# Turning mLSTM score blocks two steps behind instead of one, in banks of their own

## The chip, the cores and the metric

The kernel runs on one core of a Trainium2 chip. Five engines work side by side, each through its own line of instructions, in order: TensorE (PE in the profile, its weight loads PEld), VectorE (DVE), ScalarE (ACT), GpSimd (POOL) and SyncE (SP, which issues most DMAs). [...] Data lies in SBUF; TensorE writes to PSUM, which has eight banks of 128 partitions by 512 fp32 numbers. The metric is the device time of one launch in microseconds.

## The reference

One hybrid encoder block on 512 tokens of width 1024, all in fp32. RMSNorm, one wide projection, then three mixers side by side (a bidirectional mLSTM with 4 heads of 128, a neighbourhood attention, a cross-attention into 256 memory tokens), a gated merge, an output projection and a gated FFN. The change lies in the mLSTM. For one head and one direction it computes, with log gates `log_f`, `log_i` and their running sums `a` in a chunk:

```
m_j = max(a + m_prev, max_s D)          # D = a_j - a_s + log_i_s, causal
P = exp(D - m_j) * (q k^T)
inter_w = exp(a + m_prev - m_j)
num = P v + inter_w * (C_prev q)
den = sum(P) + inter_w * (n_prev q)
h = num / max(|den|, exp(-m_j))
```

The state `C, n` goes from chunk to chunk. A second scan runs on the reversed sequence, the two results are added, normalised over the head's 128 columns (RMS), scaled by a gain and gated by `sigmoid(o)`.

## The kernel before, in words

**Numbers and matmuls.** A product of two fp32 matrices is made from high and low parts: `mm3` (L212 to L215) issues three fp32r matmuls (high by high, high by low, low by high) into one PSUM bank. Weights come by DMA into `wr`, ACT copies the high part (`wh`, L195) and DVE subtracts to get the low part (`wl`, L196). A projection `proj` of 8 weight tiles is 24 matmuls of 512 columns. Transposes and a few small products are plain fp32.

**The mLSTM beside the projections.** TensorE has a stream of projections (memory query, output gate, memory keys and values, neighbourhood queries and keys, merge gates). The mLSTM is a generator, `ml_all`; a piece of it, up to the next `yield`, is set into the stream at places that a quota decides: each projection adds `RB`, `RM`, `RN` or `RATE` steps to it (L29, L30), a quarter of it at a time after some of its weight tiles. `late` is a list of functions which the next projection calls after its second, fourth or sixth tile (`flush`). Python's order gives priorities; Tile's scheduler then makes each engine's line from them, moving work that is ready earlier. `tc.issue_after(ins)` forbids it to put what is traced inside ahead of `ins` on that engine.

**A head.** The sequence is four blocks J of 128 tokens, both directions at once. `keys` (next head) transposes k into PSUM (L681), splits keys and queries into high and low (L689 to L694, tiles `u`) and puts `weigh` into `late`, which scales the values by their gate weights: `ew` by DVE (L699), high parts by ACT (L702), low parts by DVE (L703). `states` multiplies keys by weighted values into two banks (L721 and L213 to L215 with `at<-u`), then makes the running states C with ACT (L733) and DVE (L735) and splits them (L219, L220). Then come four steps `weights_J`, J = 0 to 3:

- scores q by k (L755) into columns 384 to 511 of a bank `ps`, and q by C (L763 for J = 0 and 3, three fp32r matmuls for J = 1 and 2) into columns 0 to 257 of the same bank;
- DVE multiplies the exponentials `E` by the scores and sums them (L771), makes the denominator and its reciprocal (L774 to L776), and mixes both directions into `ee` (L777, L778);
- the part from the state goes to H: ACT takes the first direction (L784), DVE adds the second (L786). Both read the bank `ps`.

The mixed block must be transposed before it meets the values. `turn_J` (TensorE L794, copy by ACT L795) does so inside the next block's `weights_J`, straight behind that block's scores; it writes columns 384 to 511 of its own block's bank `ps`. `values_J` (TensorE L800, DVE L801, squares by ACT L803) does the product with the values at the start of the step after, into the same columns. After a head's last block `normalise` takes the root (DVE L807, POOL L809) and four ACT scalings (L814), and `emit_y` transposes the head's H (L822), multiplies by the gate (DVE L824) and splits (L219, L220) for the branch product.

**Buffers.** PSUM is split in two pools of four banks: `mm` (projections, and the transposed keys) and `at` (blocks, states, transposed H and others). DVE and ACT also make every `wl` and `wh`, in the same lines as the mLSTM's work.

The functions as they were:

Of the kernel before, what the change touches and what calls it, by code (L numbers as in the profile page):

```python
# [17 lines left out]
P = 128  # L18
S = 512
# [9 lines left out]
WARM = 14  # L29
RM, RB, RN = 0.7, 1.25, 1.35  # L30
RATE = 1.0
# [79 lines left out]
def hybrid_block(ctx, tc, xg, xT, memT, wflat, vecs, gbias, nabias, outa, outb, outc):  # L111
# [27 lines left out]
    def mmps():  # L139
        return mmp.tile([P, 512], F32, tag="mm", name=nm("mm"))  # L140
# [519 lines left out]
    def ml_all():  # L660
# [15 lines left out]

        def keys(h, R, ee):

            pt = mmps()
            for J in range(NT):  # L680
# [10 lines left out]
            qs = qT[:, h * S + P:h * S + 3 * P]  # L691
            A.activation(q[0], qs, AF.Copy)
            V.tensor_tensor(q[1], qs, q[0].bitcast(F32), op=ALU.subtract)
            A.activation(ke[:, :2 * P].rearrange("p (j c) -> p j c", j=2), pt.rearrange("p (j c) -> p j c", j=4)[:, 0:4:3, :], AF.Copy)  # L694

            def weigh():
                wt = ml["wt"]
                for d in range(2):
                    V.tensor_scalar(ew[d], va[:, 3 * d, h, 0:129], wt[:, d, 3 * d, h:h + 1], None, op0=ALU.mult)  # L699
                    for j in range(2):  # L700
                        ds, col = slice(129 * d, 129 * d + 129), wt[:, d, j + 1, h:h + 1]
                        A.activation(wh[j][:, ds], va[:, j + 1, h, 0:129], AF.Copy, scale=col)  # L702
                        st["dve"] = V.scalar_tensor_tensor(wl[j][:, ds], va[:, j + 1, h, 0:129], col,  # L703
                                                           wh[j][:, ds].bitcast(F32), op0=ALU.mult,
                                                           op1=ALU.subtract).ins

# [3 lines left out]
        def states(h, k, w, C, q, R, ee):  # L710
# [3 lines left out]
            (ke, kh, kl), (ew, wh, wl) = k, w  # L714
            pc = [atps() for _ in range(2)]
            po = (0, 130, 0, 131)
# [31 lines left out]
        def weights_J(H, ss, h, J, k, w, C, q, R, ee):  # L748
# [6 lines left out]
            PE.matmul(kq, qT[:, hs], kT[:, hs], start=True, stop=True)  # L755
            if open_J:
                turn_J(*open_J[0])
            if len(ds) == 2:
# [23 lines left out]
            for d in ds:  # L782
                if src is None:
                    A.activation(H[:, js], pi[:, d, 0:128], AF.Copy, scale=r[:, d:d + 1])  # L784
                else:
                    V.scalar_tensor_tensor(H[:, js], pi[:, d, 0:128], r[:, d:d + 1], src, op0=ALU.mult, op1=ALU.add)  # L786
                src = H[:, js]
            if J < NT - 1:
                exps(h, J + 1, R)
            return H, ss, h, J, E, ps  # L790

        def turn_J(H, ss, h, J, E, ps):
            pt = ps[:, 384:512]
            PE.transpose(pt, E[:, 0, :], ident)  # L794
            A.activation(E[:, 1, :], pt, AF.Copy)  # L795

        def values_J(H, ss, h, J, E, ps):
            js = slice(J * P, (J + 1) * P)
            pv = ps[:, 384:512]
            PE.matmul(pv, E[:, 1, :], va[:, J, h, 0:128], start=True, stop=True)  # L800
            V.tensor_tensor(H[:, js], pv, H[:, js], op=ALU.add)  # L801
            sq = scr(128)
            A.activation(sq, H[:, js], AF.Square, accum_out=ss[:, J:J + 1])  # L803

        def normalise(H, ss):
# [4 lines left out]

            def scale():
                for J in range(NT):
                    js = slice(J * P, (J + 1) * P)
                    A.activation(H[:, js], H[:, js], AF.Copy, scale=rs[:, J:J + 1])  # L814

            late.append(scale)

        def emit_y(h, H):
            pt = atps()
            for J in range(NT):  # L820
# [8 lines left out]

        prev = None  # L830
        open_J, ahead = [], []

        def keyed(h):
            return keys(h, nxt, tp.tile([P, S], F32, tag="H", name=nm("ee"), bufs=4))

# [3 lines left out]
        for h in range(4):  # L839
            if prev:  # L840
                values_J(*open_J.pop(0))
                turn_J(*open_J[0])
            states(h, *st_h)
# [9 lines left out]
            yield  # L853
            if prev:
                values_J(*open_J.pop(0))
                normalise(*prev)
            last = prev
            prev = tp.tile([P, S], F32, tag="H", name=nm("H"), bufs=4), tiny(4)
            open_J.append(weights_J(*prev, h, 0, *own))
            yield  # L860
            for J in range(1, NT):
                if J > 1:
                    values_J(*open_J.pop(0))
                if J == 2 and last:
                    emit_y(h - 1, last[0])
                open_J.append(weights_J(*prev, h, J, *own))
                if J == 3 and h < 3:
                    st_h = keyed(h + 1)
                if J < 3 and h < 3:
                    late.append(lambda d=J - 1, n=nxt, i=st["mix"]: mask(n, d, i))  # L870
                yield
        values_J(*open_J.pop(0))
        turn_J(*open_J[0])
        yield
        values_J(*open_J.pop(0))
        normalise(*prev)
        flush()
        yield
# [654 lines left out]
```

## Time and profile before

| what | value |
|---|---|
| median of three runs | 875.74 us (875.68 to 875.85) |
| the profiled execution's own time | 876.06 us |
| its span in the trace | 874.3 us |
| lying around the span (start and end) | 1.8 us |
| granted TensorE clock | 0.999 |
| mLSTM's blocks on TensorE | from 128 us to 240 us of the span |

A row of the timeline has the start and the duration in us, engine, line, operation, tiles (out<-in), shape and count, and in brackets idle time of the engine before it with what ended it. TensorE's matmuls are pipelined and the profile models their ends, so rows overlap: the time that TensorE gives to an instruction is read from start to start. In the page's first part each engine has its busy time, the share of the span and the number of instructions.

### The profile page before, as it was taken

What the parts mean: (1) busy time and instruction counts of PE and PEld (TensorE: products, weight loads), DVE (VectorE), ACT (ScalarE), POOL (GpSimd) and SP (SyncE); (2) the same over time, 40 slices, a digit from 0 to 9 for tenths busy, and PEclk for the clock granted to TensorE, in tenths of its full rate; (3) what the DMA queues carried; (4) which work ended last, traced back from release to release, by engine and by line L of the source; (5) the groups of instructions that cost most, each with busy time, mean ns of one, the idle gap of its engine ahead of it and who ended that gap; (6) DMA issues with size and microseconds to landing.
All of it is one profiled execution on the core that took longest, in us unless ns stands there. A gap on an engine that the chain in (4) does not pass through costs nothing.

```text
span 874.3 us, 12280 instructions
## 1 busy us (share of the span) xinstructions
PE 868.3 (99%) x4287; PEld 734.8 (84%) x4287; DVE 600.8 (69%) x1332; ACT 469.8 (54%) x989; POOL 124.9 (14%) x201
## 2 busy tenths in 40 slices
PE   9999999999999999999999999999999999999997
PEld 7898888888888888888888888888888888888887
DVE  6794698987577758897676558776633466666534
ACT  7563567765456658888544455444422344444532
POOL 0101100000073470700000002111100011111010
PEclk9999999999999999999999999999999999999999
DMA  8324644522352453633223432322233322232412
GB/s 280 101 73 146 200 138 120 171 73 87 107 126 86 107 165 109 157 117 125 97 97 109 144 109 96 98 96 97 76 100 101 110 97 97 96 97 91 134 42 97
DMA packets 39422, 99.82 MB, mean 114 GB/s; under 512 B 5688, under 2 KB 13880, under 8 KB 39360
## 3 DMA queue, kind: packets, MB, share of 16 engines
q1 hardware_dynamic: 31568, 92.32, 32.5%
q0 software_dynamic: 7360, 6.32, 3.5%
q8 instruction: 34, 0.56, 0.3%
q10 hardware_dynamic: 432, 0.39, 0.1%
q14 instruction: 28, 0.23, 0.1%
HBM read 94.80 MB, written 4.21 MB: 113 GB/s over the span
## 4 chain that ended last, share of the span: by engine, by line
PE 95%; DVE 2%; ACT 1%; issue 1%; POOL 0%; POOLq 0%; ACTq 0%; DVEq 0%
PE mm L213 28%; PE mm L214 28%; PE mm L215 28%; PE at L214 2%; PE at L213 2%; PE at L215 2%; PE at L961 1%; PE at L942 1%; PE at L923 0%; PE at L924 0%; PE at L1049 0%; PE at L800 0%; DVE wl L196 0%; PE at L243 0%; PE at L794 0%
## 5 line engine op out<-in xcount | busy, mean ns | idle before, releaser
L213 PE MATMUL mm<-u,wh 128*128 128x512 f32 (+1 forms) x1072 | 414.7, 387 | 0.0
L214 PE MATMUL mm<-u,wh 128*128 128x512 f32 (+1 forms) x1072 | 412.0, 384 | 0.0
L215 PE MATMUL mm<-u,wl 128*128 128x512 f32 (+1 forms) x1072 | 411.8, 384 | 0.0
L195 ACT ACTIVATE wh<-wr 128x512 fp32r<-128x512 f32 (+2 forms) x298 | 183.9, 621 | 204.1 <-PE mm L214 161.1
L196 DVE TENSOR_TENSOR wl<-wr,wh 128x512 fp32r<-128x512 f32 (+3 forms) x300 | 204.2, 682 | 89.9 <-ACT wh L195 87.7
L215 PEld LDWEIGHTS mm<-u,wl 128*128 128x128 f32 x1072 | 201.5, 188 | 40.2 <-DVE wl L196 0.2
L214 PEld LDWEIGHTS mm<-u,wh 128*128 128x128 f32 x1072 | 201.8, 188 | 38.6 <-DVE u L220 0.3
L213 PEld LDWEIGHTS mm<-u,wh 128*128 128x128 f32 x1072 | 201.7, 188 | 38.4
L1397 POOL TENSOR_TENSOR s<-s,rb 128x512 f32<-128x512 f32 x22 | 38.0, 1730 | 402.7 <-DVE s L1396 239.0
L540 POOL DMA_DIRECT2D u<-nav_d x128 | 62.2, 513 | 64.7 <-PE at L961 22.9
L219 ACT ACTIVATE u<-s 128x512 fp32r<-128x512 f32 x26 | 16.4, 633 | 57.8 <-DVE s L1400 56.2
L1400 DVE TENSOR_TENSOR s<-mm,s 128x512 f32<-128x512 f32 x22 | 15.2, 691 | 23.9 <-POOL s L1397 23.9
L460 ACT ACTIVATE s<-pad,vec 128x512 f32<-128x512 f32 x30 | 24.4, 813 | 9.7 <-DVE pad L458 9.7
L220 DVE SCALAR_TENSOR_TENSOR u<-s,u 128x512 fp32r<-128x512 f32 x26 | 19.1, 734 | 13.5 <-ACT u L219 13.3
L461 DVE SCALAR_TENSOR_TENSOR s<-pad,vec,s 128x512 f32<-128x512 f32 x30 | 22.5, 750 | 5.5 <-ACT s L460 5.5
L1396 DVE SCALAR_TENSOR_TENSOR s<-s,s 128x512 f32<-128x512 f32 x22 | 15.2, 692 | 13.4 <-ACT s L1395 13.3
L462 DVE SCALAR_TENSOR_TENSOR s<-pad,vec,s 128x512 f32<-128x512 f32 x30 | 22.5, 750 | 0.9
L1395 ACT ACTIVATE s<-s 128x512 f32<-128x512 f32 x22 | 13.9, 632 | 14.9 <-DVE s L1394 14.9
L458 DVE TENSOR_TENSOR pad<-mm,rb 128x512 f32<-128x512 f32 x22 | 15.1, 690 | 6.4 <-PE mm L215 6.2
L1175 DVE TENSOR_TENSOR s<-mm,rb_x 128x512 f32<-128x512 f32 x16 | 11.0, 689 | 12.1 <-PE mm L215 12.0
L1407 DVE TENSOR_TENSOR u<-mm,u 128x512 f32<-128x512 f32 x13 | 9.0, 692 | 14.6 <-PE mm L215 14.6
L213 PE MATMUL mm<-wh,u 128*128 128x512 f32 x48 | 18.8, 392 | 0.0
(338 smaller groups left out, 1074.0 us busy)
## 6 DMA issues: line engine op xcount, KB each, us to landing
wr<-wflat SPq DMA_DIRECT2D x141, 512.0 KB, 3.4
nab<-nabias SPq DMA_DIRECT2D x16, 256.0 KB, 2.7
u<-nav_d POOLq DMA_DIRECT2D x128, 32.0 KB, 2.9
s<-xT SPq DMA_DIRECT2D x15, 256.0 KB, 4.0
wr<-wflat SPq DMA_DIRECT2D x14, 192.0 KB, 2.4
nav_d<-nv POOLq DMA_DIRECT2D x8, 256.0 KB, 2.5
R<-rd SPq DMA_DIRECT2D x8, 256.0 KB, 5.4
wr<-wflat SPq DMA_DIRECT2D x2, 544.0 KB, 3.4
```

The costliest lines, as they stand in the source:

```text
L195: A.activation(h[:, u:v], src, AF.Copy)
L196: V.tensor_tensor(l[:, u:v], src, h[:, u:v].bitcast(F32), op=ALU.subtract)
L213: PE.matmul(ps, lh, rh, start=start, stop=False)
L214: PE.matmul(ps, lh, rl, start=False, stop=False)
L215: st["mm"] = PE.matmul(ps, ll, rh, start=False, stop=stop).ins
L219: A.activation(h, src, AF.Copy, scale=scale)
L220: V.scalar_tensor_tensor(l, src, scale, h.bitcast(F32), op0=ALU.mult, op1=ALU.subtract)
L460: A.activation(t1, pad[:, 0:512], AF.Identity, scale=vcol(w, i), bias=vcol(b, i))
L461: V.scalar_tensor_tensor(t1, pad[:, 1:513], vcol(w, n + i), t1, op0=ALU.mult, op1=ALU.add)
L462: V.scalar_tensor_tensor(t1, pad[:, 2:514], vcol(w, 2 * n + i), t1, op0=ALU.mult, op1=ALU.add)
L540: G.dma_start(vw[r * 32:(r + 1) * 32, i * 256:(i + 1) * 256], nav_v[hf, r, CW[b]:CW[b] + 32, hp * 256:(hp + 1) * 256])
L1397: G.tensor_tensor(c, c, rb2, op=ALU.mult)
```

## The change

`turn_J` no longer takes the last block. A counter `clock` goes up with every step of the generator after the first; each block is kept with the count at which it was made, and is turned when it is at least two counts old. `values_J` follows one step behind the turn. A turned block gets an `at` bank of its own (transpose in columns 0 to 127, values in 128 to 255) and no longer uses the scores' bank. The banks of `states` and of `emit_y` come from `mm` in place of `at`. `normalise` moves from the next head's J = 0 to its J = 1 and `emit_y` from J = 2 to J = 3, where it stands ahead of the next head's `keys`; the four scalings of H are put behind J = 1's L784 (now L789) on ACT. The next head's split of the queries and its scalings are kept behind places of J = 1: on ACT behind that same L789, on DVE behind J = 1's last mix (L778, now L783). The generator has one step more at its end, and `RN` goes from 1.35 to 1.475, over 8 projections one step more. No instruction is added or taken away on any engine.

```diff
-RM, RB, RN = 0.7, 1.25, 1.35
+RM, RB, RN = 0.7, 1.25, 1.475
...
-        def keys(h, R, ee):
+        def keys(h, R, ee, act=None, dve=None):
+
+            behind = lambda ins: tc.issue_after(ins) if ins else nullcontext()
...
-            A.activation(q[0], qs, AF.Copy)
-            V.tensor_tensor(q[1], qs, q[0].bitcast(F32), op=ALU.subtract)
+            with behind(act):
+                A.activation(q[0], qs, AF.Copy)
+            with behind(dve):
+                V.tensor_tensor(q[1], qs, q[0].bitcast(F32), op=ALU.subtract)
...
-                    V.tensor_scalar(ew[d], va[:, 3 * d, h, 0:129], wt[:, d, 3 * d, h:h + 1], None, op0=ALU.mult)
+                    with behind(dve):
+                        V.tensor_scalar(ew[d], va[:, 3 * d, h, 0:129], wt[:, d, 3 * d, h:h + 1], None, op0=ALU.mult)
...
+                        with behind(act):
+                            A.activation(wh[j][:, ds], va[:, j + 1, h, 0:129], AF.Copy, scale=col)
+                        with behind(dve):
+                            st["dve"] = V.scalar_tensor_tensor(wl[j][:, ds], va[:, j + 1, h, 0:129], col,
...
-            pc = [atps() for _ in range(2)]
+            pc = [mmps() for _ in range(2)]
...
-            if open_J:
-                turn_J(*open_J[0])
+            turn_J()
...
-            return H, ss, h, J, E, ps
-
-        def turn_J(H, ss, h, J, E, ps):
-            pt = ps[:, 384:512]
-            PE.transpose(pt, E[:, 0, :], ident)
-            A.activation(E[:, 1, :], pt, AF.Copy)
-
-        def values_J(H, ss, h, J, E, ps):
+            open_J.append((H, ss, h, J, E, clock[0]))
+
+        def turn_J():
+            if open_J and clock[0] - open_J[0][-1] > 1:
+                *blk, _ = open_J.pop(0)
+                E = blk[-1]
+                pt = atps()
+                PE.transpose(pt[:, :P], E[:, 0, :], ident)
+                A.activation(E[:, 1, :], pt[:, :P], AF.Copy)
+                turned.append((*blk, pt))
+
+        def values_J():
+            if not turned:
+                return
+            H, ss, h, J, E, pt = turned.pop(0)
             js = slice(J * P, (J + 1) * P)
-            pv = ps[:, 384:512]
+            pv = pt[:, P:2 * P]
...
         def emit_y(h, H):
-            pt = atps()
+            pt = mmps()
...
+            for J in range(NT):
+                values_J()
+                scale = normalise(*last) if J == 1 and last else None
+                weights_J(*prev, h, J, *own)
+                if scale:
+                    late.append(lambda f=scale, i=st["inter"]: f(i))
+                if J == 1:
+                    ins = st["inter"], st["mix"]
+                if J == 3:
+                    if last:
+                        flush()
+                        emit_y(h - 1, last[0])
+                    if h < 3:
+                        st_h = keyed(h + 1, *ins)
+                if J in (1, 2) and h < 3:
+                    late.append(lambda d=J - 1, n=nxt, i=st["mix"]: mask(n, d, i))
+                yield
+                clock[0] += 1
```

The engines' lines differ only inside the mLSTM's stretch, on TensorE, DVE and ACT; SP's line is the same row for row, and POOL's differs in the place of one clearing of a buffer (L888).

Three places show what moved. In the rows `mm` and `at` are PSUM banks, `u_149` and its like hold the projections' inputs, `u_455` and `u_456` the queries and keys, the other `u` the split keys, queries and weighted values of a head, `ee` the mixed blocks.

TensorE, last head, J = 1: one projection's last matmul, the block's scores, and what stands behind them. Before:

```order
L215 MATMUL mm_2480<-u_147,wl_2379 128x512
L755 MATMUL at_2497<-u_456,u_455 128x128
L794 MATMUL at_2446<-ident,ee_2340 128x128
L213 MATMUL at_2497<-u_2346 128x258
L214 MATMUL at_2497<-u_2346 128x258
L215 MATMUL at_2497<-u_2346 128x258
L213 MATMUL mm_2480<-u_149,wh_2382 128x512
```

Now:

```order
L215 MATMUL mm_2484<-u_147,wl_2415 128x512
L812 MATMUL at_2443<-u_595,ee_2031 128x128
L761 MATMUL at_2499<-u_456,u_455 128x128
L213 MATMUL at_2499<-u_2327 128x258
L214 MATMUL at_2499<-u_2327 128x258
L215 MATMUL at_2499<-u_2327 128x258
L213 MATMUL mm_2484<-u_147,wh_2414 128x512
```

The turn of block 0 (L794, into block 0's own bank `at_2446`) is gone from this step; it stands in J = 2's, and here the values product (L812) of the head before it has come in.

DVE, second head, J = 3, from the low part of the keys (L690, now L691) to the last scaling for the next head's states (L703, now L709). Before:

```order
L690 TENSOR_TENSOR u_2035<-mm_2030,u_2035 128x256
L774 SCALAR_TENSOR_TENSOR y_2018<-y_2018 128x2
L196 TENSOR_TENSOR wl_2055<-wr_1971,wh_2054 128x512
L775 TENSOR_TENSOR y_2018<-y_2018,em 128x2
L699 TENSOR_SCALAR s_2036<-u_595,wt 128x129
L776 RECIPROCAL y_2018<-y_2018 128x2
L703 SCALAR_TENSOR_TENSOR u_2035<-u_595,wt,u_2035 128x129
L777 TENSOR_SCALAR ee_1632<-E_1968,y_2018 128x128
L780 TENSOR_TENSOR y_2018<-num,y_2018 128x1
L196 TENSOR_TENSOR wl_2059<-wr_1971,wh_2058 128x512
L778 SCALAR_TENSOR_TENSOR ee_1632<-E_1968,y_2018,ee_1632 128x128
L703 SCALAR_TENSOR_TENSOR u_2035<-u_595,wt,u_2035 128x129 x2
```

Now, from the split of the head's gated output (L220) on:

```order
L220 SCALAR_TENSOR_TENSOR u_2028<-s_2025,u_2027 128x512
L780 TENSOR_TENSOR y_2003<-y_2003,em 128x2
L196 TENSOR_TENSOR wl_2057<-wr_1955,wh_2056 128x512
L781 RECIPROCAL y_2003<-y_2003 128x2
L691 TENSOR_TENSOR u_2037<-mm_2032,u_2037 128x256
L782 TENSOR_SCALAR ee_1628<-E_1952,y_2003 128x128
L785 TENSOR_TENSOR y_2003<-num,y_2003 128x1
L696 TENSOR_TENSOR u_2037<-u_455,u_2037 128x256
L783 SCALAR_TENSOR_TENSOR ee_1628<-E_1952,y_2003,ee_1628 128x128
L196 TENSOR_TENSOR wl_2061<-wr_1955,wh_2060 128x512
L709 SCALAR_TENSOR_TENSOR u_2037<-u_595,wt,u_2037 128x129 x4
L813 TENSOR_TENSOR H_1796<-at_1999,H_1796 128x128
```

Before, one of the four scalings and the queries' low part stood some 18 rows ahead of this piece, in J = 2; now all four and the queries' low part (L696) stand here, behind the gated output's two DVE operations, which were in J = 2.

ACT, the same place. Before, from the gated output's high part (L219) on:

```order
L219 ACTIVATE u_1945<-s_1943 128x512
L692 ACTIVATE u_2035<-u_455 128x256
L702 ACTIVATE u_2035<-u_595,wt 128x129 x3
L195 ACTIVATE wh_1995<-wr_1912 128x512
L195 ACTIVATE wh_1999<-wr_1912 128x512
L702 ACTIVATE u_2035<-u_595,wt 128x129
L1142 ACTIVATE u_1645<-mm_1866,rc_m 128x512
```

Now:

```order
L219 ACTIVATE u_2027<-s_2025 128x512
L195 ACTIVATE wh_2056<-wr_1955 128x512
L690 ACTIVATE u_2037<-mm_2032 128x256
L694 ACTIVATE u_2037<-u_455 128x256
L1158 ACTIVATE u_1641<-mm_1859,rc_m 128x512
L195 ACTIVATE wh_2060<-wr_1955 128x512
L697 ACTIVATE s_2038<-mm_2032 128x256
L789 ACTIVATE H_1796<-at_1997,y_2003 128x128
L707 ACTIVATE u_2037<-u_595,wt 128x129 x4
```

Before, the scalings (L702) were made in J = 2, ahead of the next keys; now the four (L707) are the last of ACT's work in J = 3.

61 lines of the change are left out of this document (23 added, 38 removed).

## The prediction

> **What bounds the kernel.** I read the page's first part and its chain first, then the view of what the turn (L794) and TensorE's other instructions waited for, and last TensorE's timeline, row by row, in the stretch that the change reorders. The first part and the chain:
>
> ```profile
> PE 868.3 (99%) x4287; PEld 734.8 (84%) x4287; DVE 600.8 (69%) x1332; ACT 469.8 (54%) x989; POOL 124.9 (14%) x201
> ...
> PE 95%; DVE 2%; ACT 1%; issue 1%; POOL 0%; POOLq 0%; ACTq 0%; DVEq 0%
> ```
>
> TensorE is busy for 868.3 of 874.3 us, and the chain that ends last is 95% its own work. The change takes no instruction from TensorE, so it can win only what TensorE stands still, and only where the order differs, from 128 to 240 us. It can lose wherever DVE or ACT get something TensorE needs later than now. The view of L794 gives what ended the idle time before it (us, times; the weight load's idle time counts too, which can lie beside the matmul before it):
>
> ```profile
>   ACT H L784: 1.4, 4
>   DVE H L786: 0.6, 2
> ```
>
> Six of 16 turns find the bank occupied, for 2.0 us in all, and each time it is the reading of H that ends the wait. The view of TensorE's waits adds one for the first head's product with the state:
>
> ```profile
> PE at L763 <- DVE C L735: 0.3, 1, 0.3
> ```
>
> Together 2.3 us: the upper bound of what there is to win. Why a turn waits is seen at the first of them, in DVE's and ACT's rows:
>
> ```profile
> 132.92 0.35 DVE L778 SCALAR_TENSOR_TENSOR ee<-E,y,ee 128x128 f32<-128x128 f32 x1
> ```
>
> ```profile
> 134.73 0.35 ACT L784 ACTIVATE H<-at,y 128x128 f32<-128x128 f32 x1
> ```
>
> The mixed block was finished at 133.27, but ACT read the bank for H until 135.08, and the turn, which writes to other columns of that bank, begins at 135.13. So the input was 1.86 us early, and the bank was late.
>
> **The gain, from start to start.** How much TensorE itself lost I take from the distance between an instruction ahead of the wait and the one behind it, against the same pair where nothing was late. The first is the product with the state, L755 to the projection's L213 behind L763, late and then undisturbed:
>
> ```profile
> 128.20 0.38 PE L755 MATMUL at<-u,u 128*128 128x128 f32 x2
> ...
> 129.11 0.48 PE L213 MATMUL mm<-u,wh 128*128 128x512 f32 x1
> ...
> 155.38 0.39 PE L755 MATMUL at<-u,u 128*128 128x128 f32 x2
> ...
> 155.75 0.36 PE L213 MATMUL mm<-u,wh 128*128 128x256 f32 x1
> ```
>
> 0.91 against 0.37: 0.54 us lost. The turns, with an undisturbed one at 142.06 and another at 217.10:
>
> ```profile
> 134.74 0.40 PE L213 MATMUL mm<-u,wh 128*128 128x512 f32 x1
> 135.13 0.33 PE L794 MATMUL at<-ident,ee 128*128 128x128 f32 x1
> 135.22 0.48 PE L214 MATMUL mm<-u,wh 128*128 128x512 f32 x1
> ...
> 141.84 0.39 PE L215 MATMUL mm<-u,wl 128*128 128x512 f32 x1
> 142.06 0.39 PE L213 MATMUL mm<-u,wh 128*128 128x512 f32 x1
> ...
> 142.32 0.47 PE L214 MATMUL mm<-u,wh 128*128 128x512 f32 x1
> ...
> 149.93 0.28 PE L214 MATMUL at<-u 128*128 128x258 f32 x1
> ...
> 150.28 0.37 PE L215 MATMUL at<-u 128*128 128x258 f32 x1
> ...
> 171.69 0.40 PE L214 MATMUL mm<-wl,u 128*128 128x512 f32 x1
> ...
> 172.18 0.47 PE L215 MATMUL mm<-wh,u 128*128 128x512 f32 x1
> ...
> 211.12 0.38 PE L755 MATMUL at<-u,u 128*128 128x128 f32 x2
> 211.81 0.32 PE L794 MATMUL at<-ident,ee 128*128 128x128 f32 x1 [0.31 <-ACT H L784]
> 211.89 0.37 PE L213 MATMUL at<-u 128*128 128x258 f32 x1
> ...
> 217.10 0.39 PE L755 MATMUL at<-u,u 128*128 128x128 f32 x2
> ...
> 217.35 0.36 PE L213 MATMUL at<-u 128*128 128x258 f32 x1
> ...
> 222.12 0.39 PE L755 MATMUL at<-u,u 128*128 128x128 f32 x2
> ...
> 222.66 0.39 PE L763 MATMUL at<-C,u 128*128 128x129 f32 x2
> ```
>
> - 134.74: 0.48 against 0.26 (142.06 to 142.32): 0.22.
> - 149.93: 0.35. Undisturbed it would be half of the 0.22 that a 512-column matmul takes (141.84 to 142.06), since it has 258 columns, and 0.04 for a turn (0.26 less 0.22), so 0.15: 0.20 lost.
> - 171.69: 0.49 against 0.26: 0.23.
> - 211.12: 0.77 against 0.25 (217.10 to 217.35): 0.52.
> - 222.12: 0.54 against the same 0.25: 0.29.
>
> The turns make 1.46 and the state 0.54, 2.00 in all. The sixth turn is not among them, and the two views allow 2.3; I take 2.1, nearer to the rows.
>
> **The change, part by part.** *Own banks, two steps.* With a bank of its own the turn (L802) waits for no reading of H, so all turn waits go. It now stands a step later than its mix; a step is 6.0 us (211.12 to 217.10), so the mix, which was 1.86 us early at the first turn, has that on top. Each step takes two of the `at` pool's four banks, so a bank comes round after two steps, 12 us after its block's scores, and H's reading, some 6 us behind them now, does not hold it. What the values (L812) wait for, ACT's copy (L803), is a step old again: nothing. The copies, sums and squares are as many as before; each moves by a step on an engine that isn't the bound: nothing, beside the place below.
>
> *The state's product of the first head.* In the new order projections lie between the states and L768, enough to cover the 0.29 of waiting. The opposite holds for the third head, where a projection's matmuls go from ahead of L768 (18 to 12, six by 0.22, 1.3 us). The rows of that wait:
>
> ```profile
> 179.76 0.34 DVE L735 SCALAR_TENSOR_TENSOR C<-C,dec,at 128x129 f32<-128x129 f32 x1
> ```
>
> ```profile
> 177.23 0.28 PE L214 MATMUL at<-u 128*128 128x258 f32 x1
> ...
> 182.03 0.39 PE L763 MATMUL at<-C,u 128*128 128x129 f32 x2
> ```
>
> The state is complete at 180.10 and used at 182.03: 1.93 early, 0.6 after the change. I put 0 (to 0.3).
>
> *Tied scalings and the later gated output.* This is the place where the change can cost. For the third head's states, the scalings (DVE's L703, now L709, and ACT's L702, now L707) come last in the second head's J = 3 now, behind the gated output, which was made a step earlier. DVE's rows for what has come ahead of the last scaling, for a mask (L675), and for the last scaling:
>
> ```profile
> 166.31 0.75 DVE L824 SCALAR_TENSOR_TENSOR s<-at,ngh,u 128x512 f32<-128x512 f32 x1
> ...
> 167.75 0.69 DVE L220 SCALAR_TENSOR_TENSOR u<-s,u 128x512 fp32r<-128x512 f32 x1
> ...
> 168.90 0.42 DVE L693 TENSOR_TENSOR u<-u,u 128x256 fp32r<-128x256 f32 x1
> ...
> 169.31 0.35 DVE L703 SCALAR_TENSOR_TENSOR u<-u,wt,u 128x129 fp32r<-128x129 f32 x1
> ...
> 172.02 0.68 DVE L675 TENSOR_TENSOR R<-R,msk 128x512 f32<-128x512 f32 x1
> ...
> 175.94 0.61 DVE L703 SCALAR_TENSOR_TENSOR u<-u,wt,u 128x129 fp32r<-128x129 f32 x2
> ```
>
> Rows of one engine overlap by some 0.08 us (175.94 plus 0.61 is 176.55; the row behind it begins at 176.47), so the first four cost 0.67, 0.61, 0.34 and 0.27: 1.89 us more ahead of the last L709. It ended at 176.55, and the states' matmul that reads it, the L214 above at 177.23, was 0.68 behind: at worst TensorE waits 1.89 less 0.68, 1.2 us. Against it stands the mask: in the trace it lies in J = 3 behind the mix, now it stands ahead of J = 3's first operation, in time that DVE has while the scores are still to come; that gives back up to 0.60 and leaves 0.6 us. How much DVE stands still in these steps is in the windows view (us, then busy time and count of PE, PEld, DVE, ACT, POOL, then clock, DMA share, GB/s):
>
> ```profile
> 172.00:198.00 26.00, 25.99 (x139) 22.16 (x139) 23.80 (x88) 17.53 (x51) 1.04 (x1) 1.00 0.28 95
> ```
>
> DVE is idle for 2.2 of 26 us, which is 0.5 in a step of 6.0 us; ACT for 8.5, 2.0 in a step, so DVE is the later of the two. Idle time of 0.5 us against 0.6 us leaves a wait of 0.1, or of 0.6 where none of it falls in the right place. I take 0.3, between them; the ends for the range are 0 and 1.2.
>
> ACT's row shows what the worst end would come from:
>
> ```profile
> 167.09 0.63 ACT L219 ACTIVATE u<-s 128x512 fp32r<-128x512 f32 x1 [0.44 <-DVE s L824]
> ```
>
> ACT stood 0.44 us at L219 for DVE's product, and what stood behind it had to stand too. [...]
>
> *Banks of the `mm` pool.* The states' two banks and the transposed H now come from the projections' four. A bank is given back when its last reader is done: a projection's first matmul in the second head's J = 3 now waits until ACT has read the first half of the memory values (L1158). Between the last matmul of that half and the projection stand six matmuls of 0.22, the block's scores and eight transposes, well over 1.3 us, and an ACT operation of 512 columns takes 0.63 (L219 above): nothing. The states' banks are held from 177.5 (the L214 above, ended) to 180.10, 2.6 us; the projection behind them begins later than that. I put nothing, and up to 2.6 us each at three heads for the rival below.
>
> *RN, the further step, POOL and SP.* TensorE's instructions stay the same, only spread differently; SP's order is the same, and one clearing on POOL moves, which is busy for 14%: nothing.
>
> **Sum.** 2.1 won, 0.3 lost: 1.8 us less. The profiled execution took 876.06 us (span 874.3 and 1.8 around it), 0.3 above the median of the runs, and becomes 874.3; against the median, 875.74 less 1.8 is 873.9. About 0.2%, 1.75 us, is what a measurement can tell from no change, so this forecast lies on that edge.
>
> **The rivals.**
> - *A, the forecast:* 1.75 to 2.3 us less, 873.4 to 874.0. For it: the six waits all end with a reading of the bank that the turn no longer uses.
> - *B, the preparation comes late:* the third head's states wait the whole 1.2 us, and its product with the state 0.3; 2.1 less 1.5 leaves 0.6, 875.1 (with smaller shares of it 874.0 to 875.6). [...] For it: DVE is the fuller engine, 92% in these steps. Against it: the mask and the 0.5 us of idle time.
> - *C, nothing is won:* TensorE wins the turns and then stands at the next late operand, a low part of weights (L196 on DVE), since DVE has the same work to do in less time. The 1.8 would come back but for some 0.2: 875.5. For it: the same 92%. Against it: in the page's costliest groups the loads of L215, which take what L196 makes, waited for it only 0.2 us in the whole span (the last column), though DVE was as full in these steps before:
>
> ```profile
> L215 PEld LDWEIGHTS mm<-u,wl 128*128 128x128 f32 x1072 | 201.5, 188 | 40.2 <-DVE wl L196 0.2
> ```
>
> - *D, slower:* the `mm` pool becomes the bound. A projection that wants the bank the states hold stands until the last L741 has read it. At three heads, half of 2.6 us on the mean is 3.9; less the 1.8 it is 2.1 slower, 877.8. It decides from 1.2 us per head, where the loss passes 3.55 (1.8 and 1.75). For it: its four banks now carry the projections in flight, two states, the keys and H. Against it: the states' matmuls stand in the middle of a projection, 12 matmuls of 0.22, 2.6 us, ahead of the next one's begin.
>
> **How the numbers follow.** A 0.52, B 0.26, C 0.09, D 0.13. A alone is faster by over 0.2%: 0.52; B and C lie within it: 0.35; D slower: 0.13. The range reaches from A's lower end, 873.4, over B and C to 875.7, which leaves out D and the fringes; A's own range is 873.4 to 874.0.
>
> **What would show it.** Right: no idle time ahead of L802 for an ACT or DVE reading of H; L768 of the first head without its 0.29; TensorE's rows between 128 and 240 us shifted by 1.8. Wrong, B: idle time at the states' L213 or L214 ended by L707 or L709 around 176. Wrong, D: idle time at a projection's first L213, ended by L741, L739 or L837. Wrong, C: idle time at L215 ended by L196.

## The result and the profile after

| | before | after |
|---|---|---|
| median, run side by side | 875.80 us (875.68 to 876.27, 13 runs) | 873.78 us (873.43 to 874.44, 13 runs) |
| ratio, 95% interval | | 0.9978 (0.9969 to 0.9986) |
| profiled execution, span | 876.06, 874.3 us | 873.57, 871.8 us |

The change wins 2.0 us, 0.22%; 1.8 were forecast. The page's first part and the chain of the changed kernel:

```profile
PE 866.4 (99%) x4287; PEld 734.3 (84%) x4287; DVE 601.1 (69%) x1332; ACT 470.9 (54%) x989; POOL 124.9 (14%) x201
...
PE 98%; DVE 1%; issue 0%; ACT 0%; POOL 0%; POOLq 0%
```

DVE and ACT do the same work; the chain, 95% TensorE before, is 98% TensorE now. The view of what the turn waited for (L802) has no line under its heading, where that of L794 had 2.0 us:

```profile
its engine sat idle before it (us, times) until:
who waited for it (us, times):
```

To see how much of it belongs to the reordered stretch, I take two instructions of TensorE that stand outside it in both kernels: L612's four transposes ahead of it, and the first eight transposes of the neighbourhood attention behind it (L1049, now L1065). Before, in TensorE's timeline:

```profile
116.16 0.51 PE L612 MATMUL at<-ident,s 100*128 100x100 f32 x4
...
252.90 1.03 PE L1049 MATMUL at<-ident,s 128*128 128x128 f32 x8
```

After:

```profile
115.38 0.51 PE L612 MATMUL at<-ident,s 100*128 100x100 f32 x4
...
250.38 1.03 PE L1065 MATMUL at<-ident,s 128*128 128x128 f32 x8
```

136.74 us before, 135.00 after: 1.74 us. Of the 2.5 us by which the two spans differ, another 0.78 lie ahead of L612, where both kernels have the same rows; behind L1065 nothing is left (621.4 in both). The experiments are compared by this "stretch". Each kernel has one trace, so how well a stretch repeats is not measured; the piece behind it, which has the same instructions in every kernel here, takes 621.4 us in all 14 traces.

Three of the places after. The first head's product with the state, and the turn of 211 us:

```profile
127.42 0.38 PE L761 MATMUL at<-u,u 128*128 128x128 f32 x2
127.56 0.48 PE L213 MATMUL mm<-u,wh 128*128 128x512 f32 x1
...
128.34 0.45 PE L768 MATMUL at<-C,u 128*128 128x129 f32 x2
128.55 0.48 PE L213 MATMUL mm<-u,wh 128*128 128x512 f32 x1
...
211.25 0.38 PE L761 MATMUL at<-u,u 128*128 128x128 f32 x2
211.47 0.27 PE L802 MATMUL at<-ident,ee 128*128 128x128 f32 x1
211.50 0.36 PE L213 MATMUL at<-u 128*128 128x258 f32 x1
211.70 0.28 PE L214 MATMUL at<-u 128*128 128x258 f32 x1
211.82 0.28 PE L215 MATMUL at<-u 128*128 128x258 f32 x1
```

The turn takes 0.25 from L761 to L213, as the undisturbed one did, in place of 0.77. L768 takes 0.21 (128.34 to 128.55), in place of 0.15 undisturbed (155.60 to 155.75 before); a projection's tile (three matmuls, 127.56 to 128.34) stands between its scores and it now. The third head's states:

```profile
174.35 0.68 PE L213 MATMUL mm<-u 128*128 128x258 f32 x2
174.87 0.40 PE L213 MATMUL mm<-u,wh 128*128 128x512 f32 x1
175.11 0.28 PE L214 MATMUL mm<-u 128*128 128x258 f32 x1
```

ACT's and DVE's rows of the scalings that these matmuls read:

```profile
173.31 1.28 ACT L707 ACTIVATE u<-u,wt 128x129 fp32r<-128x129 f32 x4
```

```profile
173.88 1.14 DVE L709 SCALAR_TENSOR_TENSOR u<-u,wt,u 128x129 fp32r<-128x129 f32 x4
```

The two L213 take 0.52, where the first behind plain fp32 takes 0.20 and the next 0.12 (211.50 to 211.82 above): 0.2 us of waiting, for ACT's last scaling, which ends at 174.59. DVE's four end at 175.02, and the first L214, the kind that reads them, begins at 175.11, just in time.

### The profile page after: what moved, and what is told of

Read it like the earlier page. It is cut to its first block, busy times and chain, and to the rows that moved or that the text cites. A ratio compares the mean times of both kernels' runs of the same rounds, so it can differ in the third digit from the quotient of the medians.

```text
span 871.8 us, 12279 instructions
## 1 busy us (share of the span) xinstructions
PE 866.4 (99%) x4287; PEld 734.3 (84%) x4287; DVE 601.1 (69%) x1332; ACT 470.9 (54%) x989; POOL 124.9 (14%) x201
## 4 chain that ended last, share of the span: by engine, by line
PE 98%; DVE 1%; issue 0%; ACT 0%; POOL 0%; POOLq 0%
PE mm L213 29%; PE mm L215 29%; PE mm L214 29%; PE at L214 2%; PE at L213 2%; PE at L215 2%; PE at L977 1%; PE at L958 1%; PE at L939 0%; PE at L940 0%; PE at L761 0%; PE at L812 0%; PE at L1065 0%; PE at L243 0%; PE mm L422 0%
## 5 line engine op out<-in xcount | busy, mean ns | idle before, releaser
L213 PE MATMUL mm<-u,wh 128*128 128x512 f32 (+1 forms) x1072 | 415.2, 387 | 0.0
L215 PE MATMUL mm<-u,wl 128*128 128x512 f32 (+1 forms) x1072 | 412.3, 385 | 0.0
L214 PE MATMUL mm<-u,wh 128*128 128x512 f32 (+1 forms) x1072 | 412.2, 385 | 0.0
L196 DVE TENSOR_TENSOR wl<-wr,wh 128x512 fp32r<-128x512 f32 (+3 forms) x300 | 204.1, 682 | 90.1 <-ACT wh L195 87.6
L215 PEld LDWEIGHTS mm<-u,wl 128*128 128x128 f32 x1072 | 201.5, 188 | 40.0
L214 PEld LDWEIGHTS mm<-u,wh 128*128 128x128 f32 x1072 | 201.7, 188 | 38.7 <-DVE u L220 0.3
L213 PEld LDWEIGHTS mm<-u,wh 128*128 128x128 f32 x1072 | 201.6, 188 | 38.1
L219 ACT ACTIVATE u<-s 128x512 fp32r<-128x512 f32 x26 | 16.4, 632 | 58.7 <-DVE s L1416 56.2
L220 DVE SCALAR_TENSOR_TENSOR u<-s,u 128x512 fp32r<-128x512 f32 x26 | 19.1, 734 | 13.5 <-ACT u L219 13.3
L213 PE MATMUL mm<-wh,u 128*128 128x512 f32 x48 | 18.9, 393 | 0.0
```

The costliest lines, as they stand in the source:

```text
L196: V.tensor_tensor(l[:, u:v], src, h[:, u:v].bitcast(F32), op=ALU.subtract)
L213: PE.matmul(ps, lh, rh, start=start, stop=False)
L214: PE.matmul(ps, lh, rl, start=False, stop=False)
L215: st["mm"] = PE.matmul(ps, ll, rh, start=False, stop=stop).ins
L219: A.activation(h, src, AF.Copy, scale=scale)
L220: V.scalar_tensor_tensor(l, src, scale, h.bitcast(F32), op0=ALU.mult, op1=ALU.subtract)
```

## The experiments

All are measured by the stretch from L612 to the eight transposes (135.00 us for the change, 136.74 before), and by the median of their runs. The kernel before was run again beside each group of experiments; its medians lie between 875.73 and 875.81 us. Taken against it, the medians agree with the stretches within 0.3 us, but for RN as before. The starts of the two rows of TensorE that give a stretch stand in the table.

| kernel | L612 at | eight transposes at | stretch, us | against the change | median, us |
|---|---|---|---|---|---|
| before | 116.16 | 252.90 | 136.74 | +1.74 | 875.80 |
| the change | 115.38 | 250.38 | 135.00 |  | 873.78 |
| own banks alone | 115.69 | 251.49 | 135.80 | +0.80 | 874.98 |
| two steps without own banks | 116.06 | 250.98 | 134.92 | -0.08 | 874.13 |
| states, output in `at` | 115.38 | 250.87 | 135.49 | +0.49 | 874.70 |
| the last two together | 115.54 | 250.98 | 135.44 | +0.44 | 874.48 |
| no ties | 116.12 | 252.43 | 136.31 | +1.31 | 875.39 |
| only H's scalings untied | 116.35 | 252.00 | 135.65 | +0.65 | 874.46 |
| ties alone, on before | 115.63 | 252.29 | 136.66 | +1.66 | 875.90 |
| output in J = 2 | 115.54 | 250.87 | 135.33 | +0.33 | 874.54 |
| RN as before | 115.51 | 252.30 | 136.79 | +1.79 | 877.58 |
| spare transposes, grouped | 115.77 | 252.31 | 136.54 | +1.54 | 875.70 |
| spare transposes, apart | 116.21 | 254.00 | 137.79 | +2.79 | 876.96 |
| turn apart | 115.67 | 252.39 | 136.72 | +1.72 | 875.54 |

### Own banks, one step behind

```diff
         def turn_J(H, ss, h, J, E, ps):     # of before
-            pt = ps[:, 384:512]
+            own = atps()
+            pt = own[:, 0:P]
...
-            pv = ps[:, 384:512]
+            pv = own_pt.pop(0)[:, P:2 * P]
```

> The kernel before, with one thing of the change: a turned block gets an at bank of its own; it is still turned one step behind, and states and the gated output stay in the at pool. Theory T1 (a turn waits for the bank, not for its mix): the waits for H's readings are gone; at 211.81 the mix itself (L778, ended 211.67) leaves 0.38 of the 0.52 us, and the first state's product keeps its 0.54; so about 1.1 us less than before, near 874.7, with L778 as what ends the last turn's wait. Rival T2 (the waits are really for the mix, two steps are needed): waits stay with L778 as their end, less than 0.4 us won, 875.4 or more. Rival T3 (four at banks don't carry blocks, turned blocks and states together): new waits of TensorE at the scores or the turn for a bank, slower than before.

The stretch is 0.94 us shorter than before, where about 1.1 was expected; the median is 874.98 (ratio 0.9990, 0.9981 to 0.9999). The view of the turn (L795 there), the turn of 210.63 with its neighbours, and the weight load of another turn:

```profile
  DVE ee L778: 0.6, 2
```

```profile
210.04 0.38 PE L755 MATMUL at<-u,u 128*128 128x128 f32 x2
210.63 0.33 PE L795 MATMUL at<-ident,ee 128*128 128x128 f32 x1 [0.21 <-DVE ee L778]
210.71 0.37 PE L213 MATMUL at<-u 128*128 128x258 f32 x1
```

```profile
170.94 0.14 PEld L795 LDWEIGHTS at<-ident,ee 128*128 128x128 f32 x1 [0.30 <-PE mm L681]
```

T1 holds: no reading of H ends a wait any more. But two turns still wait, one of them surely for the mix itself. It is that of 210.63, which the view counts twice, by its weight load (0.40) and its matmul (0.21): 0.67 against 0.25, 0.42 of the former 0.52. The other is that of 171, where the profile names TensorE's own L681, which had ended at 170.73; its mix (DVE's L778) was finished only at 170.83, so the mix is the likelier cause. For these two the bank was not the only thing late, and a further step is needed. No wait for a bank (T3) shows.

### Two steps behind, in the block's own bank

```diff
-                pt = atps()
-                PE.transpose(pt[:, :P], E[:, 0, :], ident)
+                pt = ps[:, 384:512]       # the block's bank, kept in open_J
+                PE.transpose(pt, E[:, 0, :], ident)
...
-            pv = pt[:, P:2 * P]
+            pv = ps[:, 384:512]
```

> The changed kernel, but the turn writes to its own block's score bank again (columns 384 to 511, values too), two steps behind. T1: H has been read a step earlier, so no turn waits; own banks add nothing to the two steps; the same time as the changed kernel within 0.3 us, 873.5 to 874.1. Rival T2' (both are needed): a bank is now held over three steps, and the scores of the block four steps on wait for it: idle time at the scores (L761), 0.5 us or more slower than the changed kernel, 874.3 or above.

134.92, as the change; the ratio to before is 0.9980 (0.9971 to 0.9989). The view of the turn (L801 there) has no line under its heading. Two steps take all turn waits without own banks; own banks on top of them bring nothing. By the median it is 0.35 slower than the change, by the stretch 0.08 faster: no difference that these runs show.

### The states' and the output's banks back in `at`

```diff
-            pc = [mmps() for _ in range(2)]
+            pc = [atps() for _ in range(2)]
...
         def emit_y(h, H):
-            pt = mmps()
+            pt = atps()
```

> The changed kernel, with the banks of the states and of the gated output taken from the at pool as before. T1 with pools: each step takes two at banks (scores, turned block), and the two of the states and one of the output come on top, so scores or turns wait for the states' last reader (L741, about 2.6 us after the states) at three heads: 0.5 to 3 us slower than the changed kernel, 874.3 to 876.8, with idle time at L761, L802 or L727. Rival: the readers are always in time, no wait, only a different count of changes between fp32 and fp32r on TensorE (32 against 29): 0.3 us slower, 874.1.

```profile
148.11 0.28 PE L214 MATMUL at<-u 128*128 128x258 f32 x1
148.43 0.49 PE L727 MATMUL at<-ee,s 128*128 128x129 f32 x2
148.67 0.36 PE L215 MATMUL at<-u 128*128 128x258 f32 x1
```

0.49 longer, at the lower end of the expected 0.5 to 3 us. At 148 TensorE waits for the states' second bank: the second L727 was set behind other matmuls and still begins 0.32 behind an L214 that takes 0.12 elsewhere. The view of L727 has what it waited for:

```profile
  ACT H L789: 0.2, 1
```

H's reading of a block's bank is again what TensorE stands for. The other 0.3 is not divided up here; the three more changes from fp32 to fp32r do not account for it, at 0.02 each (the spare transposes below).

> Two steps behind with the turn in the block's own bank (as two_steps), and the banks of the states and the output from the at pool as before; ties and RN as in the changed kernel. T1 with pools (the waits of at_banks came from two at banks per step on top of the states'): with one bank per step there is no wait, only 32 changes from fp32 to fp32r in place of 29, 0.26 us: 135.2 for the stretch (134.92 with two_steps, 135.49 with at_banks). Rival (the states' banks are what is late in any case): 135.5 or more, idle time at L727.

That kernel has both edits. It is 135.44, no better than with own banks, against the 135.2 expected: the two banks of the states cost about 0.5 in the `at` pool whether the turned blocks have banks of their own or not. The rival had the size, but not the place: the view of L727 has no idle time there. What shows is a second wait at the product with the state (the view of L768 has "DVE C L741: 0.5, 2" there, where two steps without own banks have "0.2, 1"). It is the second head's, whose second L727 (150.55) stands 2.9 us behind the first (147.69); from `mm` the two follow each other (148.20 and 148.43). How the half us divides stays open.

### The ties

Without both ties (the next head's and H's), and without H's alone:

```diff
-                    late.append(lambda f=scale, i=st["inter"]: f(i))
+                    late.append(scale)
...
-                        st_h = keyed(h + 1, *ins)
+                        st_h = keyed(h + 1)      # only in the first of the two
```

> The changed kernel without its ties: the next head's split of the queries and scalings and the four scalings of H are left to the scheduler again; the rest as in the changed kernel. The stretch of TensorE from L612's four transposes (115.38 in the changed kernel) to the eight transposes of L1065 (250.38) is compared, 135.00 us there. Theory T4 (the new wait of 0.19 us at the third head's states, 174.35 to 174.87, comes from L707 and L709 being last in J = 3): without the ties they are made earlier, the wait goes, and one change from fp32 to fp32r less (28 against 29): 134.7 to 134.9. Rival (the ties keep the scalings out of the way of H's reading and the mix): waits at turns or values in their place, 135.2 or more.

> The changed kernel without the tie of the four scalings of H; the next head's split and scalings stay tied. TensorE's order is the same. Theory T5 (the 1.31 us that go with both ties come from the next head's split and scalings): the same stretch within 0.1, 134.9 to 135.1. Rival (the scalings of H are what was in the way): 135.5 or more.

Both expectations failed, and the sizes that came are those of the rivals. Without any tie the stretch is 1.31 us longer, and three quarters of the gain are gone; the ratio to before is 0.9994 (0.9985 to 1.0002). TensorE's rows:

```profile
128.12 0.38 PE L761 MATMUL at<-u,u 128*128 128x128 f32 x2
128.80 0.49 PE L768 MATMUL at<-C,u 128*128 128x129 f32 x2 [0.29 <-DVE C L741]
129.04 0.48 PE L213 MATMUL mm<-u,wh 128*128 128x512 f32 x1
...
174.92 0.27 PE L802 MATMUL at<-ident,ee 128*128 128x128 f32 x1
175.68 0.49 PE L727 MATMUL mm<-s 128*128 128x129 f32 x2 [0.49 <-ACT s L697]
```

The first head's wait for C is back, as before the change (0.92 from 128.12 to 129.04), and the third head's states wait for ACT's copy of the keys (0.76 from L802 to L727, where the change takes 0.11; 0.49 of it is idle until L697 is done). The view of the turn has no line here either, so the waits are not at the turns, where the first rival expected them. TensorE's order at the first head is the old one again: L768 straight behind its scores, without the projection's tile that stands between them in the change. DVE's rows there, in this kernel:

```profile
127.88 0.34 DVE L741 SCALAR_TENSOR_TENSOR C<-C,dec,mm 128x129 f32<-128x129 f32 x1
128.14 0.35 DVE L709 SCALAR_TENSOR_TENSOR u<-u,wt,u 128x129 fp32r<-128x129 f32 x1
128.40 0.34 DVE L741 SCALAR_TENSOR_TENSOR C<-C,dec,mm 128x129 f32<-128x129 f32 x1
```

And in the change:

```profile
126.70 0.69 DVE L196 TENSOR_TENSOR wl<-wr,wh 128x512 fp32r<-128x512 f32 x1
...
127.90 0.34 DVE L741 SCALAR_TENSOR_TENSOR C<-C,dec,mm 128x129 f32<-128x129 f32 x1
```

Without ties, the next head's scalings, not needed for another four steps, stand between the steps of this head's C. With them DVE makes the low part of weights (L196) there, which a projection's tile needs. C is not finished sooner: 12.9 us behind L612 in the change (128.24), 12.6 here (128.74). But TensorE has the tile to do meanwhile. That the ties are what brings the tile there is shown; by which of its rules the scheduler does it is not.

Without H's tie alone it is 135.65: half of the 1.31. TensorE's order is the same; the fourth head's states wait there, for a scaling (L703) that DVE makes behind the gated output:

```profile
198.46 0.27 PE L802 MATMUL at<-ident,ee 128*128 128x128 f32 x1
199.03 0.46 PE L727 MATMUL mm<-s 128*128 128x129 f32 x2 [0.29 <-DVE y L781]
```

```profile
198.60 0.28 DVE L703 TENSOR_SCALAR s<-u,wt 128x129 f32<-128x129 f32 x1
198.80 0.16 DVE L781 RECIPROCAL y<-y 128x2 f32<-128x2 f32 x1
```

The profile names the last event before the matmul, L781; the tile that L727 reads is L703's, ended at 198.88, and from that I take the wait to be for L703. This is the prediction's rival B, at another head.

### The ties alone

```diff
# on before: the ties of keys() as in the change, behind J = 1
                 if J == 3 and h < 3:
-                    st_h = keyed(h + 1)
+                    st_h = keyed(h + 1, *ins)
```

> The kernel before, with the ties of the next head's split of the queries and scalings alone (on ACT behind J = 1's reading of H, on DVE behind J = 1's mix); one step behind, old banks. Compared is the stretch of TensorE from L612's transposes to the eight transposes of the neighbourhood attention: 136.74 us before, 135.00 in the changed kernel. Theory T5 (the first head's wait for C at L763 comes from the next head's scalings standing among its L735 on DVE, and goes by the ties, not by the banks or the two steps): that wait of 0.54 us is gone, the turns still wait for H (1.46); TensorE changes from fp32 to fp32r 35 times in place of 31, 0.35: about 136.5. Rival (the ties only help together with the later output): the wait for C stays, 136.9 or more.

136.66, 0.08 shorter than before, where 136.5 was expected; the ratio to before is 1.0002 (0.9993 to 1.0010). TensorE's order at the first head is that of the change, with the tile between, and the wait for C is down to what the view of L770 (the L763 of this kernel) has:

```profile
  DVE C L742: 0.2, 1
```

But the turns, still one step behind and in the scores' bank, wait longer, as their view (L801; three turns, two of them counted by weight load and matmul) and one of them show:

```profile
  ACT H L791: 3.3, 5
```

```profile
159.67 0.40 PE L214 MATMUL mm<-wl,u 128*128 128x512 f32 x1
160.81 0.32 PE L801 MATMUL at<-ident,ee 128*128 128x128 f32 x1 [0.74 <-ACT H L791]
160.88 0.48 PE L215 MATMUL mm<-wh,u 128*128 128x512 f32 x1
```

The turn at 161 us alone loses 0.95 (1.21 from 159.67 to 160.88, where an undisturbed turn behind such a matmul takes 0.26). So T5 holds in that the ties take the wait for C away, and the gain is given back at the turns. The ties pay only with the two steps, and the two steps pay most with the ties.

### The gated output in J = 2

```diff
-                if J == 3:
-                    if last:
-                        flush()
-                        emit_y(h - 1, last[0])
+                if J == 2 and last:
+                    flush()
+                    emit_y(h - 1, last[0])
+                if J == 3:
```

> The changed kernel with the gated output (emit_y) made in J = 2 as before, in place of J = 3. T4: the two DVE operations of the output no longer stand ahead of the scalings, so the wait at the third head's states (0.19 us) goes; but TensorE changes from fp32 to fp32r 36 times in place of 29, which by 0.087 us each costs 0.6: 135.4 for the stretch from L612 to L1065 (135.00 in the changed kernel). Rival (such a change costs nothing): 134.8.

```profile
174.71 0.49 PE L213 MATMUL mm<-u 128*128 128x258 f32 x2
175.03 0.39 PE L213 MATMUL mm<-u,wh 128*128 128x512 f32 x1
```

As T4 expected, the two L213 take 0.32, so the wait of 0.2 us is gone, and the stretch is still 0.33 longer (0.4 expected). But the seven more changes from fp32 to fp32r are not what makes it so. In the view of H's transposes (L835) stands a wait that the change does not have:

```profile
  ACT H L827: 0.8, 3
```

A step earlier, the transposes come too soon behind ACT's scalings of H. The first head's output costs 0.25 more than in the change, the third head's 0.28, and both stand for L827. The second head's, for which TensorE does not wait, costs the same as in the change (0.43 against 0.44), though it stands alone among fp32r matmuls. 0.25 and 0.28 less the 0.2 make the 0.33.

### RN as before

```diff
-RM, RB, RN = 0.7, 1.25, 1.475
+RM, RB, RN = 0.7, 1.25, 1.35
```

> The changed kernel with RN = 1.35. The last two heads' steps lie further apart and the last output ends later; no operand gets later by it. 31 changes from fp32 to fp32r in place of 29: 0.17 us, so 135.2 for the stretch. Rival (the last output comes too late for what follows): the stretch from L1065 to the end gets longer, or 135.5 and more.

```profile
240.87 0.33 PE L835 MATMUL mm<-ident,H 128*128 128x128 f32 x1 [1.98 <-ACT H L827]
```

1.79 longer, by the rival's mechanism, the late output: with a generator step more and no higher quota, the last head's output begins right behind its normalisation. TensorE stands 2 us for ACT's scalings of H. The raised RN is what pays for the further step.

### Changes between fp32 and fp32r

```diff
                 PE.transpose(pt[:, :P], E[:, 0, :], ident)
+                PE.transpose(pt[:, 2 * P:3 * P], ident, ident)     # grouped, or, apart:
...
+                late.append(lambda: PE.transpose(pt[:, 2 * P:3 * P], ident, ident))
```

> The changed kernel with 16 spare transposes of 128 by 128 on TensorE, which nothing reads, each straight behind a turn, so that changes from fp32 to fp32r stay as they are (28 against 29). Both theories: 16 by 0.11 us more, 1.76, so 136.7 to 136.8 for the stretch from L612 to L1065; it is the base for the next.

> The same 16 spare transposes, but each in the next projection, behind its second, fourth or sixth tile: 40 changes from fp32 to fp32r in place of 28. Theory S (each costs TensorE 0.087 us): 12 by 0.087 is 1.04 more than with the transposes in a group, so 137.8 for the stretch from L612 to L1065. Rival (it costs nothing): the same as in a group within 0.2, 136.7.

One of the transposes, apart:

```profile
144.44 0.28 PE L215 MATMUL mm<-u,wl 128*128 128x256 f32 x1
144.56 0.27 PE L804 MATMUL at<-ident 128*128 128x128 f32 x1
144.58 0.36 PE L213 MATMUL mm<-u,wh 128*128 128x256 f32 x1
144.78 0.28 PE L214 MATMUL mm<-u,wh 128*128 128x256 f32 x1
```

The 16 transposes add 1.54 in a group (1.76 expected). Apart from each other they add 1.25 more, with 12 more changes, near theory S's 1.04. But the agreement is luck: the rows and the waits do not bear the theory out. The first fp32r matmul behind the transpose takes 0.20 to the next one's start, where the one ahead of it (L215) took 0.12; the transpose itself takes only 0.02. That is 0.10 for a transpose by itself, and in a group one costs 1.54 by 16, also 0.10. Up to the L214 of 144.78 two transposes have been set apart, and it lies 0.03 later behind L612 than in the grouped kernel. What costs time is waiting, as the view of L804 shows:

```profile
  ACT ee L803: 0.8, 4
```

Four of the transposes apart wait for ACT's copy of the turned block, which reads the bank that they write to; in the grouped kernel none does. Another 0.2 is a longer wait at 243 us for the last head's gated output (the L213 of 243.29 waits for L219 of ACT). Together that is 1.0 of the 1.25. What is left is 0.02 for each of the 12 changes, so theory S's 0.08 is not shown, and its rival (a change costs nothing of its own) is the nearer.

### The turn apart from the scores

```diff
-            turn_J()
+            pend.append(turn_J)
+            late.append(lambda: pend and pend.pop()())
```

> The changed kernel, but a turn is not made behind the scores: it is handed to the next projection and made after its second, fourth or sixth weight tile, by itself. TensorE changes from plain fp32 to fp32r 41 times in place of 29. Theory S (every such change costs the second fp32r matmul behind it 0.08 to 0.09 us, as in the rows 142.32 to 142.64 of before): 12 more make 1.0 us, 874.8. Rival (the change costs nothing of its own, the longer rows are only drawn longer by the profile): the same as the changed kernel within 0.3 us, 873.5 to 874.1.

This kernel computes something else: turned so late, the slot of a block holds the block two steps on, which is turned in its place. It is 1.72 longer than the change, where 1.0 was expected. The view of the values (L815 there) has "ACT ee L804: 1.0, 4", and that of the turn (L803) "ACT H L790: 0.4, 1": TensorE waits, and so the kernel says nothing on the price of a change.

## Why the prediction was right

Forecast 873.9, measured 873.78, in the case A and its own range. One of its readings is wrong from the start: it counts six turns that wait. The view of L794 counts a turn's weight load and its matmul each, and the turn of 211.81 stands in it twice, by its matmul (0.31, in the prediction's rows) and by its weight load:

```profile
211.80 0.14 PEld L794 LDWEIGHTS at<-ident,ee 128*128 128x128 f32 x1 [0.49 <-ACT H L784]
```

There is no sixth turn; the five of the rows are all. Point by point:

- **The turn waits all go.** Right, and the cause was right: without H in the way, own banks alone end three of five waits, and two steps end all.
- **The sum.** The rows' 2.00, less 0.2 at the third head's states and 0.06 at L768, make 1.74, and the stretch lost 1.74. To the hundredth that is chance, since the undisturbed pairs were read from different neighbours, which leaves the rows uncertain by 0.1 or so. The prediction went up to 2.1 for the turn that does not exist and put 0.3 where 0.26 was lost; the two errors, 0.1 and 0.04, partly cancel. The medians differ by 2.0; what they have beyond the stretch is within the scatter of single runs (873.43 to 874.44 for the change), so that 873.9 met 873.78 so closely is luck in part.
- **"Tied scalings and the later gated output", 0.3 for the third head's states.** Measured 0.2, at the place, with L707 as what was late and L709 just in time. The 1.2 us of the worst end did not come: the mask went ahead, as the prediction had it: DVE makes L675 at 168.62, ahead of J = 3's first operation (L774, 169.22).
- **The state's product of the first head.** Right, with the cause that was named: a projection's tile now lies ahead of L768 and covers the wait. What the prediction did not see is that the ties put it there; without them the same steps and banks leave the wait as it was.
- **The ties.** This is the step that failed: the prediction counted them as a cost only. They are worth 1.3 us in the new order. Without H's tie half of that goes, and the wait that comes in its place is rival B's.
- **"RN, the further step": nothing.** Right for the pair, wrong as a reason: without the higher RN the further step costs 1.8 us in the stretch. The prediction put the two in one line and did not ask what the step alone would do.
- **Banks of the `mm` pool: nothing.** Right; no projection waits for a bank, and the old pool costs 0.5 us. Rival D did not come.

## What to carry to other kernels

Where a wait ends with a reader, ask what the waiting instruction shares with it: here it was a bank, and giving the turn one step more was enough without another bank. Where an edit costs about what a theory says, look at what TensorE's weight loads waited for before believing it: three edits here seemed to price a change from fp32 to fp32r, and what they show is waits. Where a scheduler lays the lines and DVE is some 90% full (here 23.8 of the 26 us from 172 to 198 before, 23.0 after), ties that keep the next head's preparation out of the present head's way can be worth as much as the change itself, so measure the change without them, and them without the change. And a pipeline that gets one stage longer needs its quota raised with it; cost both apart, since a sum of nothing may be two terms of 2 us.

## What was not expected of the hardware

- The spare transpose of 144.56 us, plain fp32 and alone among fp32r matmuls, with no wait at it, cost TensorE 0.10 us, as much as one of the 16 in a group (1.54 by 16). The fp32r matmul behind it takes 0.08 longer to the next one's start than the one ahead of it (0.20 against 0.12), but the transpose itself takes 0.02 from start to start, where the turn of 143.07 in the same trace, among fp32 work, takes 0.11.
- L612, with the same rows ahead of it in all 14 kernels, begins between 115.38 and 116.35 us. The difference arises in the first ten us, in L431 and the projection between: from the first L422 (8.31 us in the change, 9.13 before) to L612 all 14 traces take 106.97 to 107.09 us. With one trace per kernel it stays open how much of the scatter between runs of one kernel lies there.
- With RN as before, four of nine runs took 875.5 to 875.9 us and five 877.6 to 878.0, at granted clocks of 0.999 and 0.997 to 0.998; no other kernel here has two groups. It is the only one with a standstill of 2 us in TensorE's stretch. The trace is of a run of the first group, so whether the standstill causes the lower clock stays open.
